# Another order of the down projection's products, splits prepared further ahead, and a last layer norm of two VectorE operations

## The chip, the core and the metric

The kernel runs on one core of a Trainium2 chip. Its engines work side by side, each on a queue of its own: TensorE multiplies matrices into PSUM banks, VectorE and ScalarE work elementwise, GpSimd too (not on PSUM), and SyncE (SP in the profile) starts most transfers. The metric is the device time of one execution in microseconds (us); a run's number is a median of executions.

## The reference

One step of a decoder layer, for a prompt of 1024 rows and 8 single sample rows, width 1024, in float32. Mixer, output projection and first norm come first; the change is in the feed-forward part's last third:

```python
fp = swiglu(yp * (1.0 + scp) + shp, w_up[l], w_down[l])
fs = swiglu(ys * (1.0 + scs) + shs, w_up[l], w_down[l])
yp = layer_norm(DEEPNORM_ALPHA * yp + (1.0 + gtp) * fp, ln2_w[l], ln2_b[l])
ys = layer_norm(DEEPNORM_ALPHA * ys + (1.0 + gts) * fs, ln2_w[l], ln2_b[l])

def swiglu(h, w_up, w_down):
    g, u = jnp.split(h @ w_up, 2, axis=-1)
    return (jax.nn.silu(g) * u) @ w_down
```

`layer_norm` subtracts the row's mean, multiplies by 1/sqrt(variance + 1e-5), then by the weight, and adds the bias. `w_down` is 2816 x 1024.

## The kernel before, in words

**Products.** A float32 product is made of three products of a high part and a low part of each operand (`mm3`, lines 217 to 219). A tile from memory is cast by ScalarE to the high part and VectorE subtracts to get the low part: that is a *split* (`split`, lines 1302 and 1303, tiles `d_kh` and `d_kl`).

**Down projection.** The prompt's product is done as one step of the Strassen-Winograd scheme: the 1024 rows, the 2816 inner columns and the 1024 output columns are each halved, and seven products of half size take the place of eight. P1 + P2 is the upper left block C11; with U2 = P1 + P6, the upper right is C12 = U2 + P5 + P3, the lower right C22 = U2 + P7 + P5, and the lower left C21 = U2 + P7 + P4. `FD` and `WD` hold the operands (or their sums) of each product in device memory. One product is a pass: 11 inner steps `k` (`NP`), for each of which four row tiles `tt` take three products of 128x128 by 128x512 into four PSUM banks `dn`, 132 in all. A pass whose first product starts its banks anew overwrites; the others add onto the banks of the pass before.

**Order of the passes.** `STEP` gives 1, 2, 6, 7, 5, 3, 4. Passes 1, 6, 5 and 4 take fresh banks. At the end of a pass, four VectorE adds (`dn_first`; a ScalarE copy after pass 1) bring the banks and earlier partial results together in the page tiles `PU` (`pu(q, tt)`), printed as `p`, `u` and `c` in the profile.

**Norm.** `Z[t]` holds row tile t (0 to 3 upper half, 4 to 7 lower half, "s" the samples) with the residual. `z_put(t, hf, src)` multiplies half hf of a partial result by the gate (tile `zt`, line 1583) and adds it to `Z` (line 1584). `ln_part` takes statistics of a half (line 1178), `ln_scale` aggregates them (1183), adds epsilon (1184) and raises to -0.5 on GpSimd (1185, tile `lrs`). `ln2` is the last norm: `ln_norm` makes the bias -mean x scale on VectorE (1196), ScalarE normalises the row (1198), and weight and bias are applied by VectorE on one half of the columns and by GpSimd on the other (line 1736, list `SLOW`); the last tile is cut in three parts (`FAST`). Then SP stores the tile (1740, or 1738 for the parts). `ln2` is a generator: its first step ends with the normalised row, its second with the store.

**What sets the order.** `dn_prep(n)` starts the loads of the passes' operands up to `n + LEAD` steps (lines 1519 and 1520, tile `dr`, one pair of transfers per step) and the splits up to `n`, counted along `ORD`, the list of (pass, k). It is called with n + 2 in each step; in pass 3 with 2 + k // 2; in the last pass with k + 7. Work of the norm is put in the queue `later`, and one entry is taken after each step (two in the last pass). The last pass is in `finish`: the first `KM` inner steps run over all four row tiles, and then, tile by tile, the remaining steps followed by the tile's norm, so that the four banks end one after the other. There, the program order is kept on VectorE, ScalarE and GpSimd. Elsewhere a planner orders each engine's queue when the program is built; it goes by program order as priority, by what is ready in its own model of time, and by when one of 46 pages (`N_PAGES`, 128 x 1040 float32 buffers, which hold all of `dr`, `d_kh`, `d_kl`, `Z`, `PU`) is free. On the chip each engine then runs its queue in that order.

In pass order, before: after pass 7, U3 goes into column half 0 of tiles 4 to 7; after pass 5, C22 into half 1 of them; after pass 3, C12 into half 1 of tiles 0 to 3, whose norm then runs in the last pass together with the samples' norm; in the last pass P4 is added to half 0 of tiles 4 to 7.

Of the kernel before, what the change touches and what calls it, by code (L numbers as in the profile page):

```python
# [34 lines left out]
WARM = 6  # L35
WPRI = 0, 30
LEAD = 6
KM = 6
AHEAD = 3, 7
ORDERED = {mybir.EngineType.DVE, mybir.EngineType.Activation, mybir.EngineType.Pool}  # L40
FAST = [(0, 416, 0), (768, 1024, 1), (416, 768, 0)]
SLOW = [(0, 512, 0), (512, 1024, 1)]


def _gammas():
# [134 lines left out]
def emit(ctx, tc, I, O):  # L180
# [7 lines left out]
    def page(name, dt=F32):  # L188
        return pp.tile([128, PAGE], dt, name=name, tag="pg", bufs=N_PAGES)
# [990 lines left out]
    def ln_scale(rows, key):  # L1180
        mv = small("lmv", [128, 2], 4)
        rs = small("lrs", [128, 2], 4)
        V.bn_aggr(mv[0:rows], lnst.pop(key)[0:rows].rearrange("p a b -> p (a b)"))
        V.tensor_scalar(rs[0:rows, 0:1], mv[0:rows, 1:2], LN_EPS, None, op0=ALU.add)
        G.tensor_tensor(out=rs[0:rows, 0:1], in0=rs[0:rows, 0:1], in1=C("mh")[0:rows, 0:1], op=ALU.pow)  # L1185
        lnrs[key] = (mv, rs)

    def ln_stats(x, rows, key):
        for j in range(2):
# [317 lines left out]
                fn(P)  # L1507


    ORD = [(p, k) for p in STEP for k in range(NP)]  # L1510
    DR, DS = {}, {}
    dn_at = [0, 0]

# [46 lines left out]
    def dn_first(p, tt, ps):  # L1560

        if p == 1:
            if tt % 2 == 0:
                PU[1, tt] = page(f"p1_{tt}")
                PU[2, tt] = page(f"u2_{tt}")
            A.copy(out=pu(1, tt), in_=ps)
        elif p == 6:
            V.tensor_tensor(out=pu(2, tt), in0=ps, in1=pu(1, tt), op=ALU.add)
        elif p == 7:
            V.tensor_tensor(out=pu(1, tt), in0=ps, in1=pu(1, tt), op=ALU.add)  # L1570
        elif p == 5 or p == 3:
            d = page(f"c{p}_{tt}") if tt % 2 == 0 else None
            if tt % 2 == 0:
                PU[p, tt] = d
            V.tensor_tensor(out=pu(p, tt), in0=ps, in1=pu(1 if p == 5 else 2, tt), op=ALU.add)

    def pu(q, tt):
        return PU[q, tt // 2 * 2][:, tt % 2 * 512:tt % 2 * 512 + 512]
# [7 lines left out]
    def ffn():  # L1586
        yield ("need", ("h2", 0))
        yield from up(0, (0,))
        yield ("need", ("h2", 1))
        done.add("ahead")  # L1590
        yield from up(0, (1,))
        for i in range(1, len(mats)):
            for n, r in enumerate(up(i, (0, 1))):
                yield r
                if i == len(mats) - 1 and n == 4:
                    wd_load(NP - 1)
                    dn_prep(-1)
                if i == len(mats) - 1 and n == 16:
                    dn_prep(0)
        HB.clear()  # L1600
        HC.clear()
        HS.clear()
        W.clear()
        f_end(NP - 1)
        wd_sums(NP - 1)
        dn_start()
        z_start()
        zs_load()
        st = page("lnstats")
        for i, key in enumerate([*range(8), "s"]):  # L1610
            lnst[key] = st[:, 12 * i:12 * i + 12].rearrange("p (a b) -> p a b", a=2)

        later = deque()

        def mms(p, k, tt, b):
            h, l = DS[p, k]
            o = tt * 128
            mm3(b, h[:, o:o + 128], l[:, o:o + 128], h[:, 512:1024], l[:, 512:1024],
                k == 0 and p in (1, 6, 5, 4), k == NP - 1, p in (2, 7, 3))

        banks = None
        for x, p in enumerate(STEP[:-1]):
            if p in (1, 6, 5):
                banks = [bank(f"dn{t}") for t in range(4)]
            for k in range(NP):
                n = x * NP + k
                dn_prep(n + 2 + (k // 2 if p == 3 else 0))
                for tt in range(4):
                    mms(p, k, tt, banks[tt])
                    yield 702  # L1630
                DS.pop((p, k))
                if n < 9:
                    z_load(n)
                if n == 2:
                    samp_z()
                if 5 <= n < 21:
                    z_affine((n - 5) // 2, (n - 5) % 2)
                elif n == 21:
                    z_affine("s", 0, 8)
                    z_affine("s", 1, 8)  # L1640
                elif later:
                    later.popleft()()
                if p == 7 and k == 0:
                    ln2wb = []
                    for nm in ("ln2_w", "ln2_b"):
                        t = page(nm + "b")
                        SP.dma_start(out=t[:, 0:1024], in_=I[nm].to_broadcast([128, 1024]))
                        ln2wb.append(t)
            for tt in range(4):
                if p == 2:  # L1650
                    z_put(tt, 0, banks[tt])
                else:
                    dn_first(p, tt, banks[tt])
            if p == 7:
                for tt in range(4):
                    later.append(lambda tt=tt: z_put(4 + tt, 0, pu(1, tt)))
            if p == 5:
                for tt in range(4):
                    later.append(lambda tt=tt: (z_put(4 + tt, 1, pu(5, tt)), ln_part(Z[4 + tt], 128, 4 + tt, 1)))
        for q in (1, 2, 5):  # L1660
            for tt in (0, 2):
                PU.pop((q, tt), None)
        later.extend(samp_ln2(ln2wb))
        yield from finish(later, mms, 6 * NP, ln2wb)

    def samp_z():
        zsb = zs_box.pop()
# [7 lines left out]
    def samp_ln2(wb):  # L1675
        tmp = zs_box[0]
        x = Z["s"]
        yield lambda: V.tensor_tensor(out=tmp[0:8, 0:1024], in0=tmp[0:8, 0:1024], in1=gates[2, "s"][0:8, 0:1024],
                                      op=ALU.mult)
        yield lambda: V.tensor_tensor(out=x[0:8, 0:1024], in0=x[0:8, 0:1024], in1=tmp[0:8, 0:1024], op=ALU.add)  # L1680
        yield lambda: [ln_part(x, 8, "s", j) for j in range(2)]
        g = ln2("s", 8, O["ys"], wb, False)
        yield lambda: next(g)
        yield lambda: next(g, None)

    def finish(later, mms, n0, wb):
        bk = [bank(f"dn{t}") for t in range(4)]

        def tail(t):
            return ln2(t, 128, O["yp"][t * 128:(t + 1) * 128, :], wb, t == 7)  # L1690

        def c12(tt):
            z_put(tt, 1, pu(3, tt))
            for j in range(2):
                ln_part(Z[tt], 128, tt, j)

        g = [tail(t) for t in range(4)]
        for kind, t in ("c0", "c1", "n0", "c2", "d0", "n1", "c3", "d1", "n2", "d2", "n3", "d3"):
            t = int(t)
            later.append((lambda t=t: c12(t)) if kind == "c" else (lambda t=t: next(g[t], None)))  # L1700
        for k in range(KM):
            dn_prep(n0 + min(NP - 1, k + 7))
            for tt in range(4):
                mms(4, k, tt, bk[tt])
                yield 702
            for _ in range(2):
                if later:
                    later.popleft()()
        while later:
            later.popleft()()  # L1710
        with tc.manual_schedule(engines=ORDERED):
            tails = []
            for tt in range(4):
                for k in range(KM, NP):
                    mms(4, k, tt, bk[tt])
                    yield 702
                z_put(4 + tt, 0, bk[tt])
                ln_part(Z[4 + tt], 128, 4 + tt, 0)
                for e in tails:
                    yield from e  # L1720
                tails = [tail(4 + tt)]
                next(tails[0])
            for e in tails:
                yield from e

    def ln2(key, rows, dst, wb, fast):
        x = Z.pop(key)
        ln_scale(rows, key)
        parts = FAST if fast else SLOW if rows > 8 else [(0, 1024, 1)]
        for p in parts if fast else [(0, 1024, 0)]:  # L1730
            ln_norm(x, rows, key, slice(p[0], p[1]))
        yield 0
        for a, b, pool in parts:
            E = G if pool else V
            for j, op in ((0, ALU.mult), (1, ALU.add)):
                E.tensor_tensor(out=x[0:rows, a:b], in0=x[0:rows, a:b], in1=wb[j][0:rows, a:b], op=op)  # L1736
            if fast:
                SP.dma_start(out=dst[:, a:b], in_=x[0:rows, a:b])
        if not fast:
            SP.dma_start(out=dst, in_=x[0:rows, 0:1024])  # L1740

    def misc_loads():
        tc.keep_in_program_order(SP.dma_start(out=sinkb, in_=I["sinks"].to_broadcast([128, 8])))
# [92 lines left out]
```

## Time and profile before

| | before |
|---|---|
| median of 3 runs (lowest, highest) | 1312.95 us (1308.7, 1313.05) |
| profiled execution: time, span | 1312.06 us, 1309.9 us |
| TensorE busy | 1221.3 us (93%) |
| VectorE busy | 890.0 us (68%) |
| ScalarE busy | 459.9 us (35%) |
| GpSimd busy | 177.5 us (14%) |
| down projection's first and last product | 1059.8 us, 1278.3 us |
| mean granted TensorE clock | 0.965 |

PE is TensorE's products, PEld its weight loads, DVE VectorE, ACT ScalarE, POOL GpSimd, SPq SyncE's queue of transfers. A row of the order of time gives the start in us from the span's start, the length in us, the engine, the line of the kernel, the operation, the tile written and those read, the shape, and in brackets how long the engine had been idle before it and what ended that. Consecutive instructions of VectorE overlap a little in the records, so their cost in a full queue is the distance of their starts. A row that gives three numbers in ns separated by strokes is the shortest, middle and longest of its kind.

### The profile page before, as it was taken

To read this page: it belongs to the slowest core of one execution; us is meant where nothing else is said; L and a number is where in the kernel's file an instruction comes from. 1 tells how busy PE (TensorE), PEld (TensorE's weight loads), DVE (VectorE), ACT (ScalarE), POOL (GpSimd) and SP (SyncE) were. 2 spreads that over 40 slices of the span, in tenths; PEclk is the share of its full clock that TensorE was granted. 3 is DMA by queue.
4 is the path that set the end of the run, shared out by engine and by line. 5 is a ranking of instruction groups with operands and counts; after the bars stand their busy time and mean duration, and the time that the engine had idled before them with its cause. 6 is when DMAs were issued, how large, how long until landed. Compare 5 with 4: busy or idle time off the path is not lost.

```text
span 1309.9 us, 20239 instructions
## 1 busy us (share of the span) xinstructions
PE 1221.3 (93%) x7922; PEld 1030.1 (79%) x7922; DVE 890.0 (68%) x1720; ACT 459.9 (35%) x823; POOL 177.5 (14%) x188
## 2 busy tenths in 40 slices
PE   8999979899999989687999999999999999999990
PEld 5877746688876666566999999999999977888880
DVE  2456675786555586856766676666766689564897
ACT  2335523335453224435232322232222345333332
POOL 0000032320003231010010110001010110000145
PEclk8999989999998989797999999999999999999995
DMA  9722477251134423212344444354443699755412
GB/s 286 230 104 65 150 240 243 64 191 55 62 113 145 161 84 136 96 46 85 128 140 136 153 154 153 117 166 153 138 156 117 218 386 333 232 176 177 145 47 100
DMA packets 144280, 199.08 MB, mean 152 GB/s; under 512 B 8155, under 2 KB 85571, under 8 KB 144168
## 3 DMA queue, kind: packets, MB, share of 16 engines
q1 hardware_dynamic: 133656, 161.37, 38.2%
q0 software_dynamic: 10528, 36.42, 7.3%
q8 instruction: 62, 1.02, 0.3%
q14 instruction: 34, 0.28, 0.1%
HBM read 155.02 MB, written 43.77 MB: 152 GB/s over the span
## 4 chain that ended last, share of the span: by engine, by line
issue 34%; PE 33%; DVE 10%; POOL 6%; DMA 2%; ACT 1%; SPq 0%; POOLq 0%; DVEq 0%; ACTq 0%
PE dn L218 4%; PE dn L219 4%; PE dn L217 4%; PE pin L217 3%; PE pin L219 3%; PE pin L218 3%; PE pout L218 2%; PE pout L219 2%; PE pout L217 2%; POOL fd L1441 1%; POOL fs L1445 1%; PE adab L876 1%; POOL ws L1474 1%; DMA dr<-fd 1%; POOL z L1736 1%
## 5 line engine op out<-in xcount | busy, mean ns | idle before, releaser
L217 PE MATMUL pin<-wh,hT 128*128 128x512 f32 (+1 forms) x320 | 128.1, 404 | 0.1
L218 PE MATMUL pin<-wl,hT 128*128 128x512 f32 (+1 forms) x320 | 124.2, 388 | 3.8 <-DVE wl L283 3.8
L219 PE MATMUL pin<-wh,hT 128*128 128x512 f32 (+1 forms) x320 | 124.1, 389 | 0.4 <-DVE hT L342 0.4
L217 PE MATMUL up<-hb,wa_h 128*128 128x256 f32 (+1 forms) x352 | 100.5, 286 | 0.5 <-ACT tp L1389 0.5
L218 PE MATMUL up<-hb,wa_h 128*128 128x256 f32 (+1 forms) x352 | 100.4, 285 | 0.0
L219 PE MATMUL up<-hb,wa_l 128*128 128x256 f32 (+1 forms) x352 | 100.1, 285 | 0.0
L217 PEld LDWEIGHTS pin<-wh,hT 128*128 128x128 f32 x320 | 60.1, 188 | 26.4 <-issue 13.7
L283 DVE TENSOR_TENSOR wl<-raw,wh 128x1024 fp32r<-128x1024 f32 (+1 forms) x62 | 73.9, 1195 | 6.1 <-PE ptp L659 3.5
L219 PEld LDWEIGHTS pin<-wh,hT 128*128 128x128 f32 x320 | 61.0, 191 | 15.3 <-DVE hT L342 1.7
L218 PEld LDWEIGHTS pin<-wl,hT 128*128 128x128 f32 x320 | 61.1, 191 | 14.2 <-DVE wl L283 4.3
L1408 ACT ACTIVATE sg<-sg 128x256 f32<-128x256 f32 (+1 forms) x66 | 27.5, 419 | 120.7 <-DVE sg L1407 120.7
L217 PEld LDWEIGHTS up<-hb,wa_h 128*128 128x128 f32 x352 | 67.3, 191 | 2.1 <-ACT tp L1389 1.0
L218 PEld LDWEIGHTS up<-hb,wa_h 128*128 128x128 f32 x352 | 67.2, 191 | 0.5 <-DVE hb L1260 0.3
L219 PEld LDWEIGHTS up<-hb,wa_l 128*128 128x128 f32 x352 | 67.2, 191 | 0.0
L218 PE MATMUL pout<-wl,mh 128*128 128x512 f32 x128 | 54.5, 426 | 13.2 <-DVE wl L283 13.2
L271 ACT CAST wh<-raw 128x1024 fp32r<-128x1024 f32 (+1 forms) x62 | 62.6, 1021 | 11.2 <-DMA raw<-in_w_in 6.4
L1441 POOL DMA_DIRECT2D fd<-sg x33 | 19.7, 598 | 278.8 <-DVE sg L1414 278.8
L217 PE MATMUL pout<-wh,mh 128*128 128x512 f32 x128 | 53.3, 424 | 4.2 <-ACT wh L271 4.2
L1413 DVE TENSOR_TENSOR uc<-up,tp 128x256 f32<-128x256 f32 x66 | 28.1, 426 | 39.5 <-PE up L219 39.4
L1407 DVE TENSOR_TENSOR sg<-up,tp 128x256 f32<-128x256 f32 (+1 forms) x66 | 27.8, 422 | 38.4 <-PE up L219 38.4
L219 PE MATMUL pout<-wh,ml 128*128 128x512 f32 x128 | 53.6, 419 | 0.0
L1185 POOL TENSOR_TENSOR lrs<-lrs,cst 128x1 f32<-128x1 f32 (+1 forms) x18 | 16.4, 918 | 274.3 <-PE dn L219 171.2
(504 smaller groups left out, 3732.1 us busy)
## 6 DMA issues: line engine op xcount, KB each, us to landing
wr<-in_w_up SPq DMA_DIRECT2D x44, 512.0 KB, 5.1
raw<-in_w_in SPq DMA_DIRECT2D x38, 512.0 KB, 3.6
adr<-in_w_ada_ffn SPq DMA_DIRECT2D x24, 512.0 KB, 3.9
wd<-in_w_down SPq DMA_DIRECT2D x22, 512.0 KB, 6.1
dr<-fs SPq DMA_DIRECT2D x44, 256.0 KB, 2.8
dr<-ws SPq DMA_DIRECT2D x44, 256.0 KB
fd<-sg POOLq DMA_DIRECT2D x33, 256.0 KB, 3.7
dr<-fd SPq DMA_DIRECT2D x33, 256.0 KB, 3.8
```

Source lines behind the costliest of these rows:

```text
L217: PE.matmul(ps, lhsT=ah, rhs=bh, start=start, stop=False, skip_group_check=onto)
L218: PE.matmul(ps, lhsT=ah, rhs=bl, start=False, stop=False, skip_group_check=onto)
L219: PE.matmul(ps, lhsT=al, rhs=bh, start=False, stop=stop, skip_group_check=onto)
L271: A.copy(out=h[:, 0:n], in_=src[:, 0:n])
L283: V.tensor_sub(out=l[:, 0:n], in0=src[:, 0:n], in1=f(h[:, 0:n]))
L876: PE.matmul(b[32 * q:32 * q + 32, :], lhsT=cT[:, k2 * 4 + q, :], rhs=rr[q // 2][:, (q % 2) * 512:(q % 2) * 512 + 512], start=k2 == 0, stop ...
L1185: G.tensor_tensor(out=rs[0:rows, 0:1], in0=rs[0:rows, 0:1], in1=C("mh")[0:rows, 0:1], op=ALU.pow)
L1407: V.tensor_tensor(out=dst, in0=ps, in1=add, op=ALU.add)
L1408: A.activation(out=dst, in_=dst, func=AF.Silu)
L1413: V.tensor_tensor(out=t, in0=ps, in1=add, op=ALU.add)
L1441: G.dma_start(out=two(d) if p == 4 else d, in_=ap)
L1445: G.dma_start(out=d.rearrange("a p c -> p a c"), in_=t[:, 0:1024].rearrange("p (a c) -> p a c", a=2))
```

## The change

- The passes go in the order 1, 2, 6, 5, 3, 7, 4 (`DSTEP`). Passes 1, 6, 5 and 7 take fresh banks; pass 3 adds onto those of 5, and 4 onto those of 7.
- `dn_first` follows: after 6, U2; after 5, U2 + P5; after 3, C12; after 7, C22. U2 goes into half 0 of tiles 4 to 7 after pass 6, and the samples' norm is queued there too. C12 and the norm of tiles 0 to 3 are queued after pass 3, and so before pass 7. C22 is put into tiles 4 to 7 in the last pass.
- `dn_prep` is called with n + 2 in the first four passes, with 2 + k // 2 in pass 3, with n + 8 in pass 7 and with k + 8 in the last.
- `KM` is 4 instead of 6.
- `ln2` no longer uses `ln_norm`: VectorE makes (x - mean) x weight in one SCALAR_TENSOR_TENSOR, and after `yield`, x scale + bias in a second. The power stays on GpSimd. The last tile's second operation is cut into two halves of 512 columns, each with a store.
- In `finish`, a tile's two operations follow its statistics at once.

```diff
-KM = 6
+KM = 4
-FAST = [(0, 416, 0), (768, 1024, 1), (416, 768, 0)]
-SLOW = [(0, 512, 0), (512, 1024, 1)]
...
-    ORD = [(p, k) for p in STEP for k in range(NP)]
+    DSTEP = (1, 2, 6, 5, 3, 7, 4)
+    ORD = [(p, k) for p in DSTEP for k in range(NP)]
...
+                PU[3, tt] = page(f"c12_{tt}")
             A.copy(out=pu(1, tt), in_=ps)
-        elif p == 6:
-            V.tensor_tensor(out=pu(2, tt), in0=ps, in1=pu(1, tt), op=ALU.add)
-        elif p == 7:
-            V.tensor_tensor(out=pu(1, tt), in0=ps, in1=pu(1, tt), op=ALU.add)
-        elif p == 5 or p == 3:
-            d = page(f"c{p}_{tt}") if tt % 2 == 0 else None
-            if tt % 2 == 0:
-                PU[p, tt] = d
-            V.tensor_tensor(out=pu(p, tt), in0=ps, in1=pu(1 if p == 5 else 2, tt), op=ALU.add)
+        else:
+            d, q = {6: (2, 1), 5: (1, 2), 3: (3, 2), 7: (1, 1)}[p]
+            V.tensor_tensor(out=pu(d, tt), in0=ps, in1=pu(q, tt), op=ALU.add)
...
-                k == 0 and p in (1, 6, 5, 4), k == NP - 1, p in (2, 7, 3))
+                k == 0 and p in (1, 6, 5, 7), k == NP - 1, p in (2, 3, 4))
...
-        for x, p in enumerate(STEP[:-1]):
-            if p in (1, 6, 5):
+        for x, p in enumerate(DSTEP[:-1]):
+            if p in (1, 6, 5, 7):
                 banks = [bank(f"dn{t}") for t in range(4)]
...
-                dn_prep(n + 2 + (k // 2 if p == 3 else 0))
+                dn_prep(n + (2, 2, 2, 2, 2 + k // 2, 8)[x])
...
-            if p == 7:
+            if p == 6:
                 for tt in range(4):
-                    later.append(lambda tt=tt: z_put(4 + tt, 0, pu(1, tt)))
-            if p == 5:
-                for tt in range(4):
-                    later.append(lambda tt=tt: (z_put(4 + tt, 1, pu(5, tt)), ln_part(Z[4 + tt], 128, 4 + tt, 1)))
...
-        later.extend(samp_ln2(ln2wb))
-        yield from finish(later, mms, 6 * NP, ln2wb)
+                    later.append(lambda tt=tt: z_put(4 + tt, 0, pu(2, tt)))
+                later.extend(samp_ln2(ln2wb))
+            if p == 3:
+                g = [ln2(t, 128, O["yp"][t * 128:(t + 1) * 128, :], ln2wb) for t in range(4)]
...
+                for kind, t in ("c0", "c1", "n0", "c2", "d0", "n1", "c3", "d1", "n2", "d2", "n3", "d3"):
+                    t = int(t)
+                    later.append((lambda t=t: c12(t)) if kind == "c" else (lambda t=t: next(g[t], None)))
+        yield from finish(later, mms, banks, ln2wb)
...
+    def finish(later, mms, bk, wb):
+
+        for tt in range(4):
+            later.append(lambda tt=tt: (z_put(4 + tt, 1, pu(1, tt)), ln_part(Z[4 + tt], 128, 4 + tt, 1)))
         for k in range(KM):
-            dn_prep(n0 + min(NP - 1, k + 7))
+            dn_prep(6 * NP + min(NP - 1, k + 8))
...
                 z_put(4 + tt, 0, bk[tt])
                 ln_part(Z[4 + tt], 128, 4 + tt, 0)
-                for e in tails:
-                    yield from e
-                tails = [tail(4 + tt)]
-                next(tails[0])
-            for e in tails:
-                yield from e
+                for r in ln2(4 + tt, 128, O["yp"][(4 + tt) * 128:(5 + tt) * 128, :], wb, 2 if tt == 3 else 1):
+                    yield 0
...
+    def ln2(key, rows, dst, wb, parts=1):
         x = Z.pop(key)
+        mv, rs = ln_scale(rows, key)
+        V.scalar_tensor_tensor(out=x[0:rows, 0:1024], in0=x[0:rows, 0:1024], scalar=mv[0:rows, 0:1],
+                               in1=wb[0][0:rows, 0:1024], op0=ALU.subtract, op1=ALU.mult)
         yield 0
+        for i in range(parts):
+            ks = slice(i * 1024 // parts, (i + 1) * 1024 // parts)
+            V.scalar_tensor_tensor(out=x[0:rows, ks], in0=x[0:rows, ks], scalar=rs[0:rows, 0:1], in1=wb[1][0:rows, ks],
+                                   op0=ALU.mult, op1=ALU.add)
+            SP.dma_start(out=dst[:, ks], in_=x[0:rows, ks])
```

More of the change, by code (lines that the diff above doesn't have):

```diff
@@ L1186, in ln_scale @@
         lnrs[key] = (mv, rs)
+        return mv, rs
     def ln_stats(x, rows, key):
@@ L1642, in ffn @@
                     later.popleft()()
-                if p == 7 and k == 0:
+                if p == 6 and k == 0:
                     ln2wb = []
@@ L1653, in ffn, with c12 @@
                     dn_first(p, tt, banks[tt])
-            if p == 7:
+            if p == 6:
                 for tt in range(4):
-                    later.append(lambda tt=tt: z_put(4 + tt, 0, pu(1, tt)))
-            if p == 5:
-                for tt in range(4):
-                    later.append(lambda tt=tt: (z_put(4 + tt, 1, pu(5, tt)), ln_part(Z[4 + tt], 128, 4 + tt, 1)))
-        for q in (1, 2, 5):
-            for tt in (0, 2):
-                PU.pop((q, tt), None)
-        later.extend(samp_ln2(ln2wb))
-        yield from finish(later, mms, 6 * NP, ln2wb)
+                    later.append(lambda tt=tt: z_put(4 + tt, 0, pu(2, tt)))
+                later.extend(samp_ln2(ln2wb))
+            if p == 3:
+                g = [ln2(t, 128, O["yp"][t * 128:(t + 1) * 128, :], ln2wb) for t in range(4)]
+                def c12(tt):
+                    z_put(tt, 1, pu(3, tt))
+                    for j in range(2):
+                        ln_part(Z[tt], 128, tt, j)
+                for kind, t in ("c0", "c1", "n0", "c2", "d0", "n1", "c3", "d1", "n2", "d2", "n3", "d3"):
+                    t = int(t)
+                    later.append((lambda t=t: c12(t)) if kind == "c" else (lambda t=t: next(g[t], None)))
+        yield from finish(later, mms, banks, ln2wb)
     def samp_z():
@@ L1681, in samp_ln2 @@
         yield lambda: [ln_part(x, 8, "s", j) for j in range(2)]
-        g = ln2("s", 8, O["ys"], wb, False)
+        g = ln2("s", 8, O["ys"], wb)
         yield lambda: next(g)
         yield lambda: next(g, None)
[L1686 to L1700, printed above, removed]
+    def finish(later, mms, bk, wb):
+        for tt in range(4):
+            later.append(lambda tt=tt: (z_put(4 + tt, 1, pu(1, tt)), ln_part(Z[4 + tt], 128, 4 + tt, 1)))
         for k in range(KM):
-            dn_prep(n0 + min(NP - 1, k + 7))
+            dn_prep(6 * NP + min(NP - 1, k + 8))
             for tt in range(4):
@@ L1711, in finish @@
         with tc.manual_schedule(engines=ORDERED):
-            tails = []
             for tt in range(4):
@@ L1718, in finish @@
                 ln_part(Z[4 + tt], 128, 4 + tt, 0)
-                for e in tails:
-                    yield from e
-                tails = [tail(4 + tt)]
-                next(tails[0])
-            for e in tails:
-                yield from e
-    def ln2(key, rows, dst, wb, fast):
+                for r in ln2(4 + tt, 128, O["yp"][(4 + tt) * 128:(5 + tt) * 128, :], wb, 2 if tt == 3 else 1):
+                    yield 0
+    def ln2(key, rows, dst, wb, parts=1):
         x = Z.pop(key)
[L1728 to L1731, printed above, removed]
+        mv, rs = ln_scale(rows, key)
+        V.scalar_tensor_tensor(out=x[0:rows, 0:1024], in0=x[0:rows, 0:1024], scalar=mv[0:rows, 0:1],
+                               in1=wb[0][0:rows, 0:1024], op0=ALU.subtract, op1=ALU.mult)
         yield 0
[L1733 to L1740, printed above, removed]
+        for i in range(parts):
[3 more added lines that the diff above has]
+            SP.dma_start(out=dst[:, ks], in_=x[0:rows, ks])
     def misc_loads():
```

## The prediction

> **What bounds the kernel now.** I read the page's 40 slices first (tenths of each that an engine is busy), then the windows of the down projection, then the order of time in its last 60 us, engine by engine.
>
> ```profile
> span 1309.9 us, 20239 instructions
> ...
> PE   8999979899999989687999999999999999999990
> ```
>
> TensorE is at 9 in nearly every slice and at 0 in the last. So there are two questions: does the change touch TensorE's part, and how much of the end without TensorE does it take away?
>
> The down projection runs in seven passes of about 31 us ("slots" one to seven here). The windows below are slots four, five and six, the second half of slot seven, and the end (columns: length, then busy us and count of PE, PEld, DVE, ACT, POOL, then the clock).
>
> ```profile
> 1155.00:1186.00 31.00, 31.00 (x137) 25.24 (x136) 21.96 (x22) 13.26 (x14) 0.00 (x0) 1.00 0.63 205
> 1186.00:1217.00 31.00, 31.00 (x136) 25.32 (x135) 15.00 (x20) 8.40 (x8) 0.00 (x0) 1.00 0.45 151
> 1217.00:1248.00 31.00, 31.00 (x136) 25.21 (x136) 28.89 (x37) 12.56 (x13) 9.24 (x3) 1.00 0.42 136
> ...
> 1263.00:1279.00 16.00, 15.67 (x68) 12.39 (x66) 14.72 (x28) 4.87 (x4) 10.76 (x10) 1.00 0.16 66
> 1279.00:1310.00 31.00, 0.00 (x0) 0.00 (x0) 24.05 (x35) 5.52 (x6) 17.44 (x15) 0.57 0.26 102
> ```
>
> TensorE never pauses from 1155 on, at full clock; VectorE is half idle in slot five (15.00 of 31) and nearly full from slot six on. After TensorE's end come 31 us of norm. Here are the handover and the cadence: the last product of the first bank, the last product of all, the first norm step on tile 4, one whole tile (6) on VectorE up to the next tile's first step, and the last instruction.
>
> ```profile
> 1267.86 0.39 PE L219 MATMUL dn<-d_10h,d_10l 128*128 128x512 f32 x1
> ...
> 1278.28 0.39 PE L219 MATMUL dn<-d_10h,d_10l 128*128 128x512 f32 x1
> ...
> 1275.19 0.68 DVE L1583 TENSOR_TENSOR zt<-dn,gate 128x512 f32<-128x512 f32 x1
> ...
> 1290.72 0.68 DVE L1583 TENSOR_TENSOR zt<-dn,gate 128x512 f32<-128x512 f32 x1
> 1291.43 0.69 DVE L1584 TENSOR_TENSOR z<-z,zt 128x512 f32<-128x512 f32 x1
> 1292.16 0.69 DVE L1178 BATCH_NORM_STATS2 lnstats<-z 128x6 f32<-128x512 f32 x1
> 1292.77 1.19 DVE L1736 TENSOR_TENSOR z<-z,ln_wb 128x512 f32<-128x512 f32 x1
> 1294.00 1.64 DVE L1736 TENSOR_TENSOR z<-z,ln_bb 128x512 f32<-128x512 f32 x1
> 1295.56 0.20 DVE L1183 BATCH_NORM_AGGREGATE lmv<-lnstats 128x2 f32<-128x12 f32 x1
> 1295.79 0.15 DVE L1184 TENSOR_SCALAR lrs<-lmv 128x1 f32<-128x1 f32 x1
> 1296.68 0.68 DVE L1583 TENSOR_TENSOR zt<-dn,gate 128x512 f32<-128x512 f32 x1
> ...
> 1306.23 0.52 DVE L1736 TENSOR_TENSOR z<-z,ln_bb 128x352 f32<-128x352 f32 x1
> ```
>
> Two things bind the end. Tile 4 starts at 1275.19 although its bank was complete at 1268.25 (1267.86 + 0.39): VectorE was still finishing tiles 0 to 3, whose second half (C12) comes out of slot six. Then the four last tiles go one behind the other at 5.96 us (1296.68 - 1290.72), so three of them end after TensorE. From the last VectorE end (1306.75) to the span's end are 3.15 us, the last store.
>
> **The change, part by part.** The profiled execution took 1312.06 us, 2.16 over its span and 0.9 below the median of 1312.95; the sum is made against it.
>
> *Same products.* Seven passes of 132 products stay; only their order changes. From the two PE rows one product takes 0.2316 us (10.42 us over 45), so I leave TensorE's end at 1278.7. Three passes still add onto the banks of the pass before (1 to 2, 5 to 3, 7 to 4), as three do now; the stall that 7 to 4 may bring is rival two. KM 4 instead of 6 moves the end of the first bank to 1278.67 - 63 x 0.2316 = 1264.1, and the four banks then end 4.86 us apart.
>
> *What moves.*
>
> ```profile
> 1241.64 1.24 ACT L1198 ACTIVATE z<-z,lrs 8x1024 f32<-8x1024 f32 x1 [11.75 <-DVE lrs L1196]
> ```
>
> C12 now comes out of slot five, so the norm of tiles 0 to 3 and their stores run in slots six and seven; U2's contribution to tiles 4 to 7 and the samples' norm move to slot four, where VectorE has 9 us free by the window, and they cost nothing there. The samples lose their ScalarE step, at which ScalarE's queue stands 11.75 us today with the casts behind it; those then come in time. Stores go from ten to nine of the prompt. SP is the subject of the last rival.
>
> *Splits.* VectorE takes its instructions in the order of its queue:
>
> ```profile
> 1197.42 1.05 ACT L1302 CAST d_2h<-dr 128x1024 fp32r<-128x1024 f32 x1 [0.76 <-DVE d_10l L1303]
> ...
> 1198.44 1.22 DVE L1303 TENSOR_TENSOR d_1l<-dr,d_1h 128x1024 fp32r<-128x1024 f32 x1
> ...
> 1215.64 1.38 DVE L1575 TENSOR_TENSOR c<-dn,p 128x512 f32<-128x512 f32 x2 [15.98 <-PE dn L219]
> ...
> 1217.00:1264.00 47.00, 26.94 (x20) 1.00 0.31 102
> ```
>
> In slot five it did the splits up to d_1 of the next pass, exactly the distance n+2 in the code, and then sat 15.98 us before the adds of that pass, with d_2h already cast. So 20 splits are left for slots six and seven (the window row of line 1303, whose spans are partly stretched by GpSimd). After the change slot five carries the distance 2 + k//2, which ends at 7: five more splits go into that idle time, and 15 are left. That is the worth of "further ahead", 5 x 1.14 = 5.7 us of VectorE in the crowded slots; the bounds are none (the buffer pages stay the limit, a lead of 2) and eight (a lead of 10, almost a whole pass).
>
> *VectorE's unit costs.*
>
> ```profile
> 1249.70 1.21 DVE L1303 TENSOR_TENSOR d_4l<-dr,d_4h 128x1024 fp32r<-128x1024 f32 x1
> 1250.84 1.21 DVE L1303 TENSOR_TENSOR d_5l<-dr,d_5h 128x1024 fp32r<-128x1024 f32 x1
> ...
> 1253.11 2.47 DVE L1575 TENSOR_TENSOR c<-dn,u 128x512 f32<-128x512 f32 x4
> ...
> L1160 DVE SCALAR_TENSOR_TENSOR xr<-xr,otmp x16: 664/681/5036, 461.0 to 575.4; 128x512 f32<-128x512 f32 x16
> ...
> L992 DVE SCALAR_TENSOR_TENSOR st<-vb,kss,st x32: 341/343/351, 185.0 to 196.0; 128x128 f32<-128x128 f32 x32
> ...
> L1185 POOL TENSOR_TENSOR lrs<-lrs,cst x18: 542/558/4276, 509.0 to 1302.0; 128x1 f32<-128x1 f32 x16, 8x1 f32<-8x1 f32 x2
> ...
> 1237.15 4.28 POOL L1185 TENSOR_TENSOR lrs<-lrs,cst 8x1 f32<-8x1 f32 x1 [171.24 <-PE dn L219]
> ...
> 1283.66 0.99 POOL L1185 TENSOR_TENSOR lrs<-lrs,cst 128x1 f32<-128x1 f32 x1
> ...
> 1282.61 1.64 DVE L1736 TENSOR_TENSOR z<-z,ln_bb 128x512 f32<-128x512 f32 x1
> ...
> 1284.68 0.16 DVE L1196 SCALAR_TENSOR_TENSOR lrs<-lmv,lrs 128x1 f32<-128x1 f32 x1 [0.44 <-POOL lrs L1185]
> ```
>
> An instruction of 1024 elements starts 1.14 us before the next; of 512, 0.60 (half the elements; the four adds give 2.47 / 4 = 0.62). A SCALAR_TENSOR_TENSOR with an immediate scalar costs what a TENSOR_TENSOR does (681 ns at 512). The new ones take their scalar per partition; L992 does too: 343 ns at 128, against 0.28 by the straight line through 0.68 and 1.21. So 0.06 more: 1.27 us long, 1.20 start to start at 1024, 0.66 and 0.74 at 512. Bounds: no extra, or twice the slope (1.07 more), which neither row supports.
>
> *The power on GpSimd stays,* and now VectorE itself waits for it. Its middle length is 0.56 us; with splits running beside it, it took 4.28 (1237.15); behind one VectorE instruction it ended 0.40 after that ended (1284.65 against 1284.25), and VectorE resumed at 1284.68. The first new operation (mean and weight) starts right behind the tiny add, so the power ends after it and the second (scale and bias) waits 0.45 at the head of VectorE's queue; splits queued behind wait too. Bounds: 0 and 0.56, its whole length. The Trainium skill, "SBUF — State Buffer", section "SBUF: two separate sides", says that GpSimd and a VectorE instruction with two SBUF inputs hold a shared port pair as an exclusive lock for the whole instruction. By it the 0.45 is paid at each tile; if the power ran beside the first operation it would be nothing, and the sum 8 x 0.45 = 3.6 us lower; the 4.28 us row agrees with the lock.
>
> *The sum from 1215.6*, where slot five's adds begin: adds of product 3, 2.5; 15 splits x 1.14, 17.1; four C12 updates of four 0.60 instructions, 9.6; four first norm steps (0.23 from the aggregate to the add, 0.15 the add, 1.20 the first operation), 6.3; four second operations 1.20 + 0.45, 6.6; adds of product 7, 2.5; four C22 updates of three 0.60 instructions, 7.2. Together 51.8, so VectorE reaches tile 4 at 1267.4, 3.3 us after its bank (1264.1) instead of 6.9. Per tile then: 0.71 + 0.73 + 0.69 (the gaps and the statistics of tile 6 above) + 0.23 + 0.15 + 1.27 + 0.45 + 1.20 = 5.43 us, slightly over the 4.86 of the banks, so VectorE stays the bound: three tiles 16.3. The last tile takes 4.23 up to its second operation, then 0.66 + 0.74: 5.6. End of VectorE 1289.3. The last store has 256 KB instead of 176:
>
> ```profile
> out_yp<-z SPq DMA_DIRECT2D x7, 512.0 KB, 2.6
> ...
> out_yp<-z SPq DMA_DIRECT2D x1, 176.0 KB, 2.0
> ```
>
> By these, 3.15 + 0.15 = 3.3: span 1292.6, time 1294.8.
>
> **The rivals.**
>
> *One: TensorE sets the end.* If VectorE isn't late (a lead of 10, or the powers cost nothing), tile 7 begins at 1278.8: 1278.8 + 5.6 + 3.3 + 2.2 = 1289.9. For it: slot five's idle time. Against: 51.8 us of work in 48.5.
>
> *Two: the adds of product 7 come late and TensorE waits for them.* They read banks that product 4 adds onto. In the queue's order 2.5 + 12 splits (13.7) + 9.6 + 6.3 + three second operations (5.0) = 37.1 us stand before them, so the first is done at 1253.4, where TensorE wants its bank near 1248. It waits 5.4, the first bank ends at 1269.5, and the rest of the chain from there gives 1269.5 + 16.3 + 5.6 + 3.3 + 2.2 = 1296.9. Against it: the planner may place them earlier.
>
> *Three: the lead of the splits does not grow.* Then 20 splits are left: 5.7 us more, 1300.5. The Trainium skill, "Perfetto Trace Analysis", section "Optimizing Scalar/DVE Operations", advises moving work off VectorE where it is saturated; this change moves the normalisation onto it. Slot six at 28.89 of 31 speaks for this rival, slot five at 15.00 against.
>
> *Four: it doesn't do what it says.* If the norms of tiles 0 to 3 still fell behind TensorE's end, four times 3.23 us (1.58 + 1.65) come back: 1307.7, no change.
>
> *Five, slower: SP's queue.* It is in order, and stores stand in it among loads:
>
> ```profile
> 1206.64 0.32 SPq L1519 DMA_DIRECT2D dr<-fd  x1
> ...
> 1231.54 0.51 SPq L1519 DMA_DIRECT2D dr<-fd  x1
> ...
> 1248.72 0.30 SPq L1740 DMA_DIRECT2D out_ys<-z  x1
> 1249.11 0.34 SPq L1519 DMA_DIRECT2D dr<-fd  x1
> ```
>
> Today the samples' store held it about 16 us with one load behind. After the change the samples' store comes in slots four to five and four tile stores in slots six and seven, with more loads behind. The first load of the last pass (1206.64) is 41 us ahead of its slot, so TensorE waits only for a hold of over 41 us, one for one. To lose the 17.3 us that I forecast takes a hold of 58 us; at 66 the time is 1320. Against it: today's 16.
>
> **How the numbers follow.** Forecast 0.38 (1294.8; its own range 1292 to 1297), rival one 0.2, two 0.2, three 0.13, four 0.05, five 0.04. The range reaches from rival one to a little over rival three, 1289 to 1301, and leaves 0.09 out, and as much again for what I mis-sized. Faster by over 0.5% (below 1306.4, about what a measurement of this kernel can tell from no change): 0.91; within: 0.05; slower: 0.04.
>
> **What the new profile would show.** Right: the first norm step on the bank of tile 4 near 1267; tiles 5.4 us apart, with a gap of about 0.45 before each second operation, released by the power; GpSimd with nothing but powers after 1215; the end without TensorE near 13 us instead of 31. Rival one shows waits of VectorE for TensorE in the last four tiles; rival two a gap of TensorE before the last pass; rival three the splits up to d_1 only before slot five's adds. The prediction is wrong if the two new operations run longer than 1.3 us, if TensorE has new waits in the earlier passes, or if a pow costs VectorE more than 0.7.

## The result, and the profile after

The changed kernel takes 1290.62 us (median of 4 runs, 1288.8 to 1291.83), the kernel before 1311.7 us beside it (1308.7 to 1313.05): ratio 0.9841, 95% interval 0.9818 to 0.9865. Forecast was 1294.8 with a range of 1289 to 1301. The profiled execution took 1291.37 us, 1.87 over its span.

The span and TensorE's line of the 40 slices on the page of the changed kernel: the last slice, 0 before, is now 6.

```profile
span 1289.5 us, 20190 instructions
...
PE   8999979899999989696999999999999998999996
```

The windows of slots four, five and six, of slot seven in two parts, and of the end (length, busy us and count of PE, PEld, DVE, ACT, POOL, then clock, DMA share, GB/s):

```profile
1155.00:1186.00 31.00, 31.00 (x136) 25.27 (x135) 28.85 (x36) 12.70 (x13) 2.61 (x1) 1.00 0.47 149
1186.00:1217.00 31.00, 31.00 (x136) 25.12 (x135) 19.32 (x20) 11.36 (x11) 0.00 (x0) 1.00 0.71 243
1217.00:1248.00 31.00, 31.00 (x136) 25.22 (x136) 31.00 (x43) 13.26 (x13) 7.51 (x4) 1.00 0.47 157
1248.00:1263.00 15.00, 15.00 (x66) 12.17 (x65) 14.54 (x20) 0.00 (x0) 1.17 (x1) 1.00 0.16 63
1263.00:1279.00 16.00, 15.86 (x69) 12.59 (x67) 13.29 (x20) 0.00 (x0) 3.98 (x3) 1.00 0.16 66
1279.00:1290.00 11.00, 0.00 (x0) 0.00 (x0) 6.25 (x9) 0.00 (x0) 1.81 (x2) 0.64 0.25 95
```

TensorE's part is untouched: busy 31.00 of 31 in each slot. VectorE's work has moved forward, from 21.96 to 28.85 us in slot four, 15.00 to 19.32 in slot five, 28.89 to 31.00 in slot six. The end without TensorE is 11 us instead of 31.

The handover and the cadence in the order of time: last product of the first bank and of all, last VectorE instruction before the four tiles, the first norm step of tiles 4, 5, 6 and 7, and the two new operations of tile 4 and the last of tile 7.

```profile
1263.96 0.39 PE L217 MATMUL dn<-d_10h,d_10l 128*128 128x512 f32 x1
...
1278.46 0.40 PE L217 MATMUL dn<-d_10h,d_10l 128*128 128x512 f32 x1
...
1261.92 0.69 DVE L1176 BATCH_NORM_STATS2 lnstats<-z 128x6 f32<-128x512 f32 x1
1264.39 0.69 DVE L1578 TENSOR_TENSOR zt<-dn,gate 128x512 f32<-128x512 f32 x1 [1.78 <-PE dn L217]
...
1266.88 1.28 DVE L1713 SCALAR_TENSOR_TENSOR z<-z,lmv,ln_wb 128x1024 f32<-128x1024 f32 x1
1268.59 1.29 DVE L1718 SCALAR_TENSOR_TENSOR z<-z,lrs,ln_bb 128x1024 f32<-128x1024 f32 x1 [0.43 <-POOL lrs L1183]
1269.80 0.68 DVE L1578 TENSOR_TENSOR zt<-dn,gate 128x512 f32<-128x512 f32 x1
...
1275.20 0.68 DVE L1578 TENSOR_TENSOR zt<-dn,gate 128x512 f32<-128x512 f32 x1
...
1280.60 0.68 DVE L1578 TENSOR_TENSOR zt<-dn,gate 128x512 f32<-128x512 f32 x1
...
1284.80 1.42 DVE L1718 SCALAR_TENSOR_TENSOR z<-z,lrs,ln_bb 128x512 f32<-128x512 f32 x2 [0.44 <-POOL lrs L1183]
```

Read against the same rows of before, the 20.4 us of span come from four places. Tile 4 starts 10.8 us earlier (1275.19 to 1264.39). Tiles 4 and 5 take 10.81 us instead of 15.53 (4.7; 4.2 of it in tile 4, with which norms of tiles 2 and 3 were interleaved before), tile 6 takes 5.40 instead of 5.96 (0.6). The last tile takes 5.62 (1280.60 to 1286.22) instead of 10.07 (4.45). The last store lands 3.28 after VectorE's end instead of 3.15 (-0.1).

### The profile page after: what moved, and what is told of

Read it like the earlier page. It is cut to its first block, busy times and chain, and to the rows that moved or that the text cites. A ratio compares the mean times of both kernels' runs of the same rounds, so it can differ in the third digit from the quotient of the medians.

```text
span 1289.5 us, 20190 instructions
## 1 busy us (share of the span) xinstructions
PE 1222.2 (95%) x7922; PEld 1031.0 (80%) x7922; DVE 883.6 (69%) x1712; ACT 449.2 (35%) x812; POOL 159.0 (12%) x170
## 4 chain that ended last, share of the span: by engine, by line
PE 37%; issue 34%; DVE 8%; POOL 5%; DMA 2%; ACT 1%; POOLq 0%; DVEq 0%; SPq 0%; ACTq 0%
PE dn L216 4%; PE dn L215 4%; PE dn L217 4%; PE pin L215 4%; PE pin L217 3%; PE pin L216 3%; PE pout L216 2%; PE pout L217 2%; PE pout L215 2%; POOL fd L1440 1%; POOL fs L1444 1%; PE adab L874 1%; POOL ws L1473 1%; DVE z L1550 1%; DMA z<-yd 1%
## 5 line engine op out<-in xcount | busy, mean ns | idle before, releaser
L1183 POOL TENSOR_TENSOR lrs<-lrs,cst 128x1 f32<-128x1 f32 (+1 forms) x18 | 23.7, 1320 | 284.0 <-DVE lrs L1182 218.9
```

## The experiments

Totals drift in a place that no kernel here touches. The row of the down projection's first products (shortest, middle and longest ns, then first and last start), from the changed kernel:

```profile
L215 PE MATMUL dn<-d_0h x4: 387/392/504, 1059.8 to 1063.2; 128*128 128x512 f32 x4
```

Over the ten profiled executions that first product comes between 1057.9 and 1063.2. So beside the ratio, which stands against the kernel before on the same chip, I give the length of the *stage*, from this product to the span's end. It is 250.1 before and 229.7 after. Each stage length is that of one profiled execution.

| run | median us | ratio to before (95%) | stage us |
|---|---|---|---|
| e0_after, changed kernel again | 1291.38 | 0.9840 (0.9825 to 0.9855) | 229.8 |
| e1_norm_only | 1302.19 | 0.9911 (0.9891 to 0.9931) | 239.8 |
| e2_order_only | 1302.79 | 0.9908 (0.9889 to 0.9926) | 240.1 |
| e3_lead2 | 1295.99 | 0.9861 (0.9843 to 0.9880) | 234.3 |
| e4_km6 | 1296.86 | 0.9869 (0.9849 to 0.9890) | 233.8 |
| e5_km3 | 1291.94 | 0.9845 (0.9831 to 0.9860) | 228.6 |
| e8_pipe_km3 | 1290.12 | 0.9836 (0.9819 to 0.9853) | 229.1 |
| e9_no_gpsimd | 1299.58 | 0.9901 (0.9883 to 0.9918) | 235.8 |

**The norm alone.** The kernel before with the new `ln2`; order, splits and `KM` stay.

```diff
 def ln2(key, rows, dst, wb, ...):
-    ln_scale; ln_norm (ScalarE); weight and bias on VectorE and GpSimd
+    mv, rs = ln_scale(rows, key)
+    V.scalar_tensor_tensor(... scalar=mv, in1=weight, op0=subtract, op1=mult)
+    V.scalar_tensor_tensor(... scalar=rs, in1=bias, op0=mult, op1=add)
 # finish
-    previous tile's second step, then next(tails[0])
+    both steps of this tile at once
```

> The kernel before with the new norm alone: old order of the products, old splits, KM 6. My theory (the gain has two parts: the order lets tile 4 start at its bank, the norm shortens every tile): C12 still comes out of slot six, so tile 4 starts late, near 1272 to 1275 us, then tiles 5.4 us apart and a last tile of 5.6; span 1273 + 16.2 + 5.6 + 3.3 = 1298, time about 1300. Rival 'norm alone': 1290.6, tile 4 no later than in the changed kernel. Rival 'order alone': 1311, as before.

Stage 239.8, 10.3 shorter than before. The first bank's last product, and the first norm step of tiles 4, 5 and 6 in it:

```profile
1271.18 0.39 PE L219 MATMUL dn<-d_10h,d_10l 128*128 128x512 f32 x1
...
1273.28 0.64 DVE L1584 TENSOR_TENSOR zt<-dn,gate 128x512 f32<-128x512 f32 x1
...
1283.22 0.68 DVE L1584 TENSOR_TENSOR zt<-dn,gate 128x512 f32<-128x512 f32 x1
...
1288.62 0.68 DVE L1584 TENSOR_TENSOR zt<-dn,gate 128x512 f32<-128x512 f32 x1
```

The cadence of 5.40 is there already. What is missing against the changed kernel is the early start: tile 4's bank is ready at 1271.57, its first step comes 1.7 later, and tile 4 then takes 9.94 us because norms of tiles 2 and 3 are still interleaved with it. In stage time its start is 5.6 us later than in the changed kernel (210.2 against 204.6) and its stretch 4.5 longer (9.94 against 5.41): the 10.1 us that order, splits and `KM` bring on top. The expectation had tile 4 start later in stage time than it did and then take 5.4 us like the others; the interleaved norms were not in it.

**Order, splits and KM alone.** The changed kernel with the old `ln2` (ScalarE, VectorE and GpSimd) and the old lag of one tile.

```diff
-    (the two SCALAR_TENSOR_TENSOR of ln2)
+    ln_scale; ln_norm (ScalarE); weight and bias on VectorE and GpSimd
 # finish
-    both steps of this tile at once
+    previous tile's second step, then next(tails[0])
```

> The changed kernel with the old norm (ScalarE normalises, VectorE and GpSimd share weight and bias, last tile in three parts): order, splits and KM 4 stay. My theory: VectorE reaches tile 4 at about its bank (1264 to 1266), then tiles 5.96 apart and a last tile of 10.07 as before: 1265.5 + 17.9 + 10.1 + 3.15 = 1296.6 span, time about 1299. Rival 'norm alone': 1311. Rival 'order alone': 1290.6.

Stage 240.1, 10.0 shorter than before. Here rival two of the prediction is seen. End of pass 7 and start of the last pass on TensorE, with ScalarE's and VectorE's rows at that time:

```profile
1250.58 0.40 PE L219 MATMUL dn<-d_10h,d_10l 128*128 128x512 f32 x1
1255.19 0.77 PE L217 MATMUL dn<-d_0h 128*128 128x512 f32 x1 [4.21 <-ACT z L1199]
...
1258.67 0.40 PE L219 MATMUL dn<-d_0h,d_0l 128*128 128x512 f32 x1
...
1253.88 1.24 ACT L1199 ACTIVATE z<-z,lrs 128x1024 f32<-128x1024 f32 x1 [1.96 <-DVE lrs L1197]
...
1254.37 2.47 DVE L1572 TENSOR_TENSOR p<-dn,p 128x512 f32<-128x512 f32 x4
...
1272.89 0.69 DVE L1580 TENSOR_TENSOR zt<-dn,gate 128x512 f32<-128x512 f32 x1 [5.18 <-PE dn L219]
```

The profile names ScalarE's `z`, which ended last (1255.12); but the product adds onto a bank, not onto `z`. What it needs is the first of the four adds of product 7, which by the 0.62 of each ends at about 1255.0; in the run without GpSimd, below, the wait at this place is put down to these adds. The adds stand behind splits and norm work in VectorE's queue. The next eight products start 0.43 us apart on the mean instead of 0.23 (1255.19 to 1258.67), another 1.6 us. The window shows it as clock:

```profile
1248.00:1263.00 15.00, 10.79 (x40) 8.43 (x39) 14.56 (x22) 3.42 (x3) 8.83 (x6) 0.89 0.26 105
```

So the first bank is 6.1 us late in stage time (210.7 against 204.6), and VectorE waits 5.18 for it. The last tile again takes 10.1 instead of 5.6, 4.45 more. These two make the difference to the changed kernel; the stall was not in the expectation, and the stage is 3.3 us longer than it had it. Norm alone (-10.3) and order alone (-10.0) sum to the whole -20.4, but not because they act on different things: without the new norm the new order runs into a stall, and without the new order the new norm starts late.

**The lead of the splits.** Rival three, put into the changed kernel.

```diff
-                dn_prep(n + (2, 2, 2, 2, 2 + k // 2, 8)[x])
+                dn_prep(n + 2)
```

> The changed kernel with a split distance of n + 2 in all six first passes (k + 8 in the last as it is). My theory: 5 or 6 splits more are left for slots six and seven, VectorE reaches tile 4 near 1268.3 instead of 1262.6, past its bank at 1264.4: 3.9 us more, time about 1294.5. Rival 'the pages set the lead, the distance nothing': 1290.6. Rival 'TensorE starves': gaps of TensorE in slots six and seven and more than 1297.

Stage 234.3, 4.6 longer than the changed kernel. The adds after slot five, the last split, and TensorE's last products on the first bank and tiles 4 and 5:

```profile
1213.98 1.39 DVE L1570 TENSOR_TENSOR c<-dn,u 128x512 f32<-128x512 f32 x2 [17.67 <-PE dn L217]
...
1263.51 1.21 DVE L1302 TENSOR_TENSOR d_10l<-dr,d_10h 128x1024 fp32r<-128x1024 f32 x1
...
1262.14 0.39 PE L215 MATMUL dn<-d_10h 128*128 128x512 f32 x1
...
1265.82 0.39 PE L217 MATMUL dn<-d_10h,d_10l 128*128 128x512 f32 x1
...
1266.24 0.69 DVE L1578 TENSOR_TENSOR zt<-dn,gate 128x512 f32<-128x512 f32 x1 [0.33 <-PE dn L217]
...
1272.59 0.68 DVE L1578 TENSOR_TENSOR zt<-dn,gate 128x512 f32<-128x512 f32 x1
```

VectorE sits 17.67 us idle before the adds, and five more splits stand in the crowded slots. The backlog reaches tile 4 in a way that I had not thought of: through the last split. `d_10l` is there at 1264.72, so the planned order puts 14 products of the second bank between the first bank's `d_10h` and its last two. TensorE does not pause, but the first bank is complete at 1266.21, 3.65 us later in stage time. The rest is C22 of tile 7, now done inside tile 4's stretch (6.35 against 5.41). The edit takes back pass 7's lead of 8 along with that of pass 3, so the 4.6 us belong to both; a run with one of them alone was not made.

**KM back at 6.**

```diff
-KM = 4
+KM = 6
```

> The changed kernel with KM 6 instead of 4. My theory (tile 4 waits for its bank, then VectorE is the bound): the first bank ends near 1268.4 instead of 1264.3, the whole chain moves with it, about 3.9 us more, time about 1294.5. Rival 'VectorE's backlog sets tile 4's start': unchanged, 1290.6. Rival 'TensorE's end sets the last tile': unchanged, 1290.6.

Stage 233.8, 4.1 longer. The first step of tile 4:

```profile
1271.98 0.69 DVE L1578 TENSOR_TENSOR zt<-dn,gate 128x512 f32<-128x512 f32 x1 [5.46 <-PE dn L217]
```

With the backlog gone VectorE waits for the bank, and the four tiles of 5.40 then run one by one past TensorE's end. `KM` 4 brings the bank 4.2 us earlier (18 products of 0.2316), and nearly all of it arrives. The new order without its leads and its `KM` was not run, so its own share of the 10.1 us is not measured.

**The changed kernel again, and KM at 3.**

> The changed kernel again, as the measure for the other three of this chip: 0.984 of the kernel before by all theories, 229.7 us from the first product of the down projection to the span's end.

Stage 229.8, against 229.7 in the first profile: 0.1 apart.

```diff
-KM = 4
+KM = 3
```

> The changed kernel with KM 3. My theory: the first bank ends 2.4 us earlier (near 1261.9), before VectorE is free (1262.6), so the chain moves by 1.8 us at most: 227.9 us from the first product of the down projection instead of 229.7, time 0.14% less, hardly more than the timing can tell. Rival 'TensorE's end sets the last tile': nothing.

Stage 228.6. First step of tiles 4, 5 and 7:

```profile
1265.12 0.69 DVE L1578 TENSOR_TENSOR zt<-dn,gate 128x512 f32<-128x512 f32 x1 [0.68 <-PE dn L217]
...
1271.47 0.68 DVE L1578 TENSOR_TENSOR zt<-dn,gate 128x512 f32<-128x512 f32 x1
...
1282.27 0.68 DVE L1578 TENSOR_TENSOR zt<-dn,gate 128x512 f32<-128x512 f32 x1
```

Tile 4 starts 2.0 earlier in stage time, but VectorE had C22 of tile 7 left, and tile 4's stretch grows from 5.41 to 6.35. Of the expected 1.8 us 1.2 remain. Tile 7 starts 0.6 after TensorE's end (1281.71): the tiles are almost bound by TensorE, as in rival one. By the ratio it is not told from the changed kernel.

**Hiding the wait for the power.** `KM` 3, and the second operation of a tile comes behind the next tile's gate product, so that the power has time.

```diff
+                V.tensor_tensor(out=tmp, in0=bk[tt], in1=gate, op=ALU.mult)
+                (second operation of the tile before)
+                V.tensor_tensor(out=x[:, 0:512], in0=x[:, 0:512], in1=tmp, op=ALU.add)
                 ln_part(x, 128, 4 + tt, 0)
+                (first operation of this tile)
```

> KM 3, and the second norm operation of a tile comes behind the next tile's gate product, so that the power on GpSimd has that time. The gate product reads one operand from PSUM and one from SBUF. My theory: the 0.43 us waits of VectorE for the power go away for three of the four tiles (1.3 us), and with KM 3 (1.8 us) the stage takes 226.6 us instead of 229.7; time about 0.24% less than the changed kernel. Rival 'any VectorE instruction holds the power up': the power ends only after the gate product and a wait of about 0.4 us stays, 227.9 us.

Stage 229.1: missed, it is no faster than `KM` 3 alone. The start of its last tile:

```profile
1277.53 0.69 DVE L1707 TENSOR_TENSOR zt<-dn,gate 128x512 f32<-128x512 f32 x1 [0.69 <-PE dn L217]
1278.13 1.28 DVE L1726 SCALAR_TENSOR_TENSOR z<-z,lrs,ln_bb 128x1024 f32<-128x1024 f32 x1
```

The waits for the power are gone in three tiles, and in their place VectorE waits for the bank. The gain turned into a new wait, and the last tile pays: tile 6's second operation (1.2) now stands inside it, 6.7 us instead of 5.6. Whether the power runs beside the gate product, one of whose inputs is in PSUM, can't be read here, since that product waited for TensorE. The profile of the kernel before shows it, at tile 4's gate product (1275.19, 0.68 us long):

```profile
1275.29 1.07 POOL L1185 TENSOR_TENSOR lrs<-lrs,cst 128x1 f32<-128x1 f32 x2 [1.44 <-DVE lrs L1184]
```

These are two powers of 0.55 us each, the length of a power alone, and the first lies inside the gate product. So the product did not hold it up.

**Without GpSimd, but with ScalarE.** The changed kernel with ScalarE normalising as before, weight and bias as two VectorE instructions of 1024, and the old lag.

```diff
-        (the two SCALAR_TENSOR_TENSOR)
+        ln_norm(x, rows, key)
         yield 0
+        V.tensor_tensor(... in1=weight, op=ALU.mult)
+        V.tensor_tensor(... in1=bias, op=ALU.add)
```

> The changed kernel with a norm of the old kind but without GpSimd's halves: ScalarE normalises, VectorE multiplies by the weight and adds the bias over the whole width; the power stays on GpSimd; the second half of the norm comes behind the next tile's statistics as in the kernel before. It tells what of the norm's gain is GpSimd's absence. If it is all GpSimd (the theory I favour): tiles about 5.4 us apart and only the last tile longer by about 1.5 us for the way over ScalarE, 231 to 232 us from the first product. Rival 'ScalarE in the chain is the cost': near the order-only kernel's 240.1 us.

Stage 235.8, between the two expectations. The start of the last pass and the last tile:

```profile
1248.54 0.47 PE L217 MATMUL dn<-d_0h 128*128 128x512 f32 x1 [2.03 <-DVE p L1572]
1248.84 0.40 PE L218 MATMUL dn<-d_0l,d_0h 128*128 128x512 f32 x1
...
1287.87 1.23 DVE L1722 TENSOR_TENSOR z<-z,ln_wb 128x1024 f32<-128x1024 f32 x1 [1.31 <-ACT z L1199]
```

Against order alone 4.3 us are won, though VectorE does the whole of weight and bias: the stall of TensorE is 2.03 instead of 4.21, the products run at full rate behind it, and the last tile takes 9.6. To the changed kernel 6.1 are still missing: 2.2 in the first bank (the stall) and 3.95 in the last tile, where tile 6's weight and bias, the power and ScalarE's step come in turn. So taking GpSimd off is worth less than half of the 10.4 us that the two operations bring here, against the expectation favoured; the rest is the step over ScalarE and the lag that it asks for.

No run here beats the changed kernel by more than the measurement tells. TensorE's end stands at 219.1 of the stage; with 5.6 for the last tile and 3.3 for its store that would be 228.0, an estimate by these rows, 1.7 under what it takes.

## Why the prediction was right, and where its sum was off

**The mechanism.** The likeliest case holds from tile 4 on, and not for its start. TensorE's end does not move (1278.86 against the 1278.7 put), the norm of tiles 0 to 3 runs ahead of it, and VectorE's own time per tile then sets the end. Tiles are 5.41, 5.40 and 5.40 apart (5.43 put), the last takes 5.62 (5.6), the landing 3.28 (3.3). Each second operation of the last four tiles starts 0.43 to 0.44 after the engine fell idle, released by the power (0.45). The new operations take 1.28 (1.27). But tile 4 was put 3.3 us behind its bank, for VectorE's sake, and it started on it. So 1291.37 us lies below the 1292 to 1297 of the likeliest case, nearer to the 1289.9 of rival one. What came, VectorE in time at tile 4 and late at tile 7, is none of the cases listed: rival one lets tile 7 begin at TensorE's end even where a lead of 10 makes VectorE early, though 5.43 a tile against 4.86 a bank, both in the prediction, carry tile 7 to 1280.4. By the prediction's own terms that case is 1264.1 + 16.3 + 5.6 + 3.3 + 2.2 = 1291.5. That the range held it is due to the two cases on either side.

**The splits.** The last one ahead of slot five's adds is `d_6`, so the lead is 7 and 15 are left, as put:

```profile
1209.11 1.22 DVE L1302 TENSOR_TENSOR d_6l<-dr,d_6h 128x1024 fp32r<-128x1024 f32 x1
1215.87 1.39 DVE L1570 TENSOR_TENSOR c<-dn,u 128x512 f32<-128x512 f32 x2 [5.54 <-PE dn L217]
```

The idle time there is 5.54 instead of 15.98. Five splits were put at 5.7 us of end; taking them back, with the lead of pass 7, cost 4.6.

**The step that failed is the sum from 1215.6.** 51.8 us were put; VectorE was done at 1262.6, 46.7 after 1215.9. Three terms were too large. First, the statistics of the first halves of tiles 0 to 3 were counted into C12 (4 x 0.60 = 2.4), but their inputs are there from the start, and they were done in slot four, one at 1172.62 and three here:

```profile
1179.58 1.86 DVE L1176 BATCH_NORM_STATS2 lnstats<-z 128x6 f32<-128x512 f32 x3
```

Second, the wait for the power was charged to tiles 0 to 3 too (4 x 0.45 = 1.8). The waits from 1215 on, grouped (total us, times, longest), and GpSimd's and VectorE's rows around the longest power:

```profile
DVE z L1718 <- POOL lrs L1183: 1.7, 4, 0.4
```
```profile
1235.20 4.33 POOL L1183 TENSOR_TENSOR lrs<-lrs,cst 128x1 f32<-128x1 f32 x1 [5.74 <-DVE lrs L1182]
...
1237.90 1.22 DVE L1302 TENSOR_TENSOR d_4l<-dr,d_4h 128x1024 fp32r<-128x1024 f32 x1
1239.04 0.69 DVE L1176 BATCH_NORM_STATS2 lnstats<-z 128x6 f32<-128x512 f32 x1
1239.64 1.27 DVE L1718 SCALAR_TENSOR_TENSOR z<-z,lrs,ln_bb 128x1024 f32<-128x1024 f32 x1
```

In this execution only the last four tiles wait. In slot six other instructions stand between a tile's two operations, and where the power took 4.33 us beside them, VectorE had work all that time. That is not sure to be so. In the second profile of the same kernel (`e0_after`) that power took 1.46 us, and the one of tile 2, 1.45 in the first profile, took 2.59; VectorE waited for it, with a split between the two operations:

```profile
1244.17 2.59 POOL L1183 TENSOR_TENSOR lrs<-lrs,cst 128x1 f32<-128x1 f32 x1 [6.81 <-DVE lrs L1182]
...
1246.80 1.28 DVE L1718 SCALAR_TENSOR_TENSOR z<-z,lrs,ln_bb 128x1024 f32<-128x1024 f32 x1 [0.43 <-POOL lrs L1183]
```

Tile 4 was not later for it: VectorE then waited 1.32 us for the bank instead of 1.78. Over the six profiles with the new order and the new norm, tiles 0 to 3 wait not at all in two, once (0.43 or 0.44) in three, and twice (0.45 and 0.31) in `e3_lead2`. So the charge of 1.8 us was too large in each. The Trainium skill, "SBUF — State Buffer", section "SBUF: two separate sides", from which the prediction took the rule of the exclusive lock, agrees with the row of 4.33: the power ends (1239.53) 0.41 after `d_4l`, the last instruction there with two inputs in SBUF. But the lock held up GpSimd, and VectorE pays for it only when its queue comes to the second operation before the power is done. Why one power gets in behind the first such instruction and another only behind the fourth, in two executions of one queue order, no run here shows. Third, a first norm step costs less in a full queue than by itself: 0.12 from aggregate to add, 0.06 for the add, 1.20, together 1.38 instead of 1.58 (0.8 for four). The three make 5.0 of the 5.1 us.

So VectorE waits 1.78 us for tile 4's bank (1264.35, 1264.1 put) instead of 3.3 us the other way, and from there the prediction's own terms give the end: 1264.4 + 16.3 + 5.6 + 3.3 = 1289.6, against 1289.5 measured. TensorE's bank thus took up part of the 5.1 us: the forecast is off by 3.1 in the span, and by 0.3 in what the time has over it (1.87 instead of 2.16).

**The rivals.** *One* holds for the start of tile 4 and for nothing after: tile 7 starts at 1280.60, 1.7 behind its bank, and there is one wait of VectorE for TensorE in the last four tiles where this rival had more. *Two* did not come in the changed kernel; VectorE's adds of product 7, and TensorE at the same place:

```profile
1246.87 0.64 DVE L1570 TENSOR_TENSOR p<-dn,p 128x512 f32<-128x512 f32 x1
...
1248.68 1.89 DVE L1570 TENSOR_TENSOR p<-dn,p 128x512 f32<-128x512 f32 x3
...
1248.19 0.39 PE L215 MATMUL dn<-d_0h 128*128 128x512 f32 x1
...
1248.88 0.40 PE L215 MATMUL dn<-d_1h 128*128 128x512 f32 x1
```

The first add was done at 1247.5, not 1253.4, ahead of two more norm steps and three splits, and TensorE took three inner steps on the first bank while the other three adds ran. It was a live danger all the same: 4.2 us in order alone, 2.0 without GpSimd. *Three*, tried together with pass 7's lead, costs 4.6 where 5.7 were put, over the late split and the late C22. *Four* is refuted by the windows and GpSimd's rows: no GpSimd work but powers from 1215 on, and 11 us of end. *Five* did not come: TensorE is busy 31.00 of 31 in slots four to six, and 30.86 of 31 in slot seven.

## What to carry to other kernels

Where one engine is full in a stretch and idle just ahead of it, look for work whose inputs are ready early; preparing splits further ahead in two passes was worth 4.6 us, and it is the scheduled slack, not the share of busy time, that shows them. Do not charge a wait on another engine in full at each place: in the full queue it came at none to two of four tiles, with up to 0.45 us each, at the serial end at every tile, with 0.44. Two changes whose single gains add up can still depend on one another, so test each alone and read which wait ended last in each.

## What was not expected of the hardware

After a gap of 4.21 us TensorE's next eight products took 3.48 us instead of 1.85, with a granted clock of 0.89 over that window; after a gap of 2.03 us the second product already came 0.30 after the first, and the third 0.24 behind it. The Trainium skill, "TensorE: Matmul & The Clock Gate", Part 1 "The HAM clock gate", says that an idle window of about 3.4 us halves the clock and that a busy one of that length restores it; both gaps here agree, and the slow stretch of 3.48 us too. So the longer stall cost more than itself: 4.2 and 1.6 us.

A power of one element per partition on GpSimd took 0.55 us by itself and beside a gate product with one input in PSUM, and 1.45 beside one VectorE operation of 1.28 with two inputs in SBUF. Where further such operations followed in the changed kernel, it took anything from 1.45 to 4.33, and not the same in two executions of one kernel (4.33 and 1.46; 1.45 and 2.59).

The start of the stage moved by 5.3 us between profiled executions of kernels whose edits all lie behind it (and the five runs of `e9_no_gpsimd` alone spread over 5.9 us), while the stage's length in the two profiles of the changed kernel differed by 0.1.
